# Gate rows, residual inputs and second-residual rows loaded some steps before use; second residual cut into eight pieces

## The chip, the cores and the metric

The kernel runs on one core of a Trainium2 chip. The metric is the device time of one execution in microseconds (us), as the median of several runs. The notation is that of the profile: PE is TensorE (matmul), PEld its weight loads, DVE is VectorE, ACT is ScalarE, POOL is GpSimd, SP is SyncE, which here only issues DMA transfers; a name with a q behind it (SPq) is the engine's own instruction queue. "L849" is line 849 of the kernel.

## The reference, cut to what matters

One encoder block over 512 positions of width 2048, in float32:

```
mod  = silu(c) @ w_ada + b_ada           # shift1, scale1, gate1, shift2, scale2, gate2, each of width 2048
z    = (x*(1+scale1) + shift1) @ w_in + b_in
mix  = (sigmoid(ga) * (A(z) @ w_a) + sigmoid(gb) * (B(z) @ w_b)) @ w_o + b_o
x    = LN1(alpha*x + gate1*mix)
x    = LN2(alpha*x + gate2*(relu((x*(1+scale2)+shift2) @ w_m1 + b_m1)**2 @ w_m2 + b_m2))
```

The part at stake is what joins the matmuls of w_o to the first matmuls of w_m1: the first residual (alpha*x + gate1*mix, with b_o folded in), its norm, and the start of the second residual (alpha*x with x the output of LN1 including its gain and bias, plus gate2*b_m2), to which the products of w_m2 are then added.

## The kernel before, in words

Every matrix is cut into blocks of 256 rows by 512 columns, and each block is one step `kp` of a group of output columns `cg`. The values are float32 kept as a pair of rounded halves (hi and lo), so that a product takes three matmuls (hi*hi, hi*lo, lo*hi). A block's way to TensorE is: SP loads it into a `wraw` buffer (512 KB, three buffers), ScalarE writes `whi` (L76), VectorE writes `wlo` (L77), three buffers each, and then come the matmuls of that step: 24 of 512 columns where four tiles of 128 positions are done, 24 of 256 columns where half the positions are done (`tok_0`, `tok_1`), 12 of 512 columns where two tiles are done. `Weights.take(k)`, called at the start of step k, gives out block k and emits the split of block k+2 and the load of a later one; so `wlo` of block k+2 stands on VectorE ahead of all that the stages of step k emit, and behind all that earlier steps emitted. Each engine works through its own queue in the order in which the program emits it, SP's transfers too.

`stages` is a table by hand: `stages={2: [f]}` calls f after the matmuls of step 2 have been emitted. The order around the change is this:

1. The last group of w_a (L773 to L778) with `parts` (splitting the mix into hi and lo pairs for w_o), then sums of the modulation vector (`mod_sum`), the last four `parts`, an activation that loads the table for the square root (L787), and small vectors for LN1.
2. `gate_rows` (L801): the columns gate1 and gate2 are copied (ScalarE, L804 and L805), turned into rows by one TensorE transpose (L807), copied from PSUM (L809) and stored to a buffer in HBM, `grow`. From there they are loaded again, spread over 128 partitions: `g1_row` (two loads of 512 KB) and `cond` (1 MB, gate2).
3. `residual(c)` (L828), for each of four column blocks c: load b_o's row (spread over the partitions, 256 KB) and x's four tiles (256 KB each), scale the row and multiply it by gate1, and add it to x, all on GpSimd: six instructions.
4. The groups c = 0 and c = 1 of w_o with four tiles (`token_dense`, L837, matmuls at L849), eight steps each, `gated_1` (L854) behind each: three VectorE instructions a tile. Then c = 2 and 3 for the first two tiles (`early`) and for the last two (`late`), with the norm and the transposes of LN1 in their stages.
5. The first group of w_m1 by halves of the positions (`tok_0`, `tok_1`, matmuls at L187), the second group (cg 1) with four tiles; `hidden` (L940) behind each: relu and square, two instructions a tile on ScalarE and two on VectorE. In the steps 0, 2, 4 and 6 of cg 1 stands `skip_path(c)` (L904) for c = 0 to 3: three rows are loaded, one product on GpSimd, nine instructions on VectorE.
6. The four groups of w_m2's first slab (L849, four steps each), then slab after slab without anything of the above.

`slot` tiles (128x512 float32, 39 buffers) hold x, rows, hidden values and intermediates alike. PSUM has 8 banks, handed out in turn.

Of the kernel before, what the change touches and what calls it, by code (L numbers as in the profile page):

```python
# [14 lines left out]
OP = mybir.AluOpType  # L15
# [3 lines left out]
P = 128  # L19
D = 2048  # L20
# [9 lines left out]
ALPHA = 2.0 ** 0.25  # L30
# [10 lines left out]
def block_kernel(ctx: ExitStack, tc: tile.TileContext, t):  # L41
    nc = tc.nc
# [11 lines left out]
    def slot(name, dt=F32):  # L54
        return heap.tile([P, 512], dt, name=name, tag="slot")

    def slot_pair(name):
        return slot(name + "h", F32R), slot(name + "l", F32R)
# [5 lines left out]
    def bank(name):  # L64
        return psum.tile([P, 512], F32, name=name, tag="bank")

    def f32(ap):
        return ap.bitcast(F32)

    def load(dst, src):  # L70
        nc.sync.dma_start(dst, src)  # L71
        return dst
# [121 lines left out]
    def dense(*args, **kw):  # L194
        out = []
        for _ in dense_steps(out, *args, **kw):
            pass
        return out
# [22 lines left out]
    cond = const.tile([P, D], F32, name="cond")  # L221
# [42 lines left out]
    grow = dram.tile([2, D], F32, name="grow")  # L264
# [354 lines left out]
    def do(f, *args):  # L619
        return lambda: f(*args)  # L620
# [24 lines left out]
    def merged(*parts):  # L645
        out = {}
        for p_ in parts:
            for k, v in p_.items():
                out.setdefault(k, []).extend(v)
        return out  # L650
# [94 lines left out]
    stages = {1 + i: [do(norm, 0, i)] for i in range(4)}  # L745
    stages.update({5: [do(norm, 1, 0)], 6: [do(norm, 1, 1), do(rows, 0)], 7: [do(norm, 1, 2), do(norm, 1, 3)]})
    sg = gate(0, 0, stages)
    for hf in range(2):
        stages = {k: [do(spatial, k // 3, i, mixed[k // 3]) for i in (2 * (k % 3) - 2, 2 * (k % 3) - 1)]
                  for k in (1, 2, 4, 5)} if hf == 0 else {}  # L750
# [12 lines left out]
    mp = []  # L763
# [6 lines left out]
    for cg in range(4):  # L770
        if cg:
            sg = gate(0, cg)
        ps = dense(t["w_a"], cg, 4, Ap,  # L773
                   stages={k: [do(parts, 3 * k + j) for j in range(3)] for k in range(4)} if cg == 3 else None)
# [23 lines left out]
    TILES = range(4)  # L798
    COLS = [slice(512 * c, 512 * (c + 1)) for c in range(4)]

    def gate_rows():  # L801

        both = small.tile([P, 2, KC], F32, name="gcols", tag="gcols")
        nc.scalar.copy(both[:, 0], mod[:, 2])  # L804
        nc.scalar.copy(both[:, 1], mod[:, 5])  # L805
        ps = bank("gT")
        nc.tensor.transpose(ps[:2 * KC, :P], both.rearrange("p g k -> p (g k)"), ident)  # L807
        rows_ = slot("gT")
        nc.scalar.copy(rows_[:2 * KC, :P], ps[:2 * KC, :P])  # L809
        for i in range(2):  # L810
            nc.sync.dma_start(grow[i].rearrange("(k p) -> k p", p=P), rows_[i * KC:(i + 1) * KC, :P])

    def row(src, name="row"):
        return load(slot(name), src.broadcast_to([P, 512]))

    gate_rows()
    g1_row = [wts.tile([P, 1024], F32, name="g1row", tag="araw") for _ in range(2)]
    for i, g in enumerate(g1_row):
        load(g, grow[0:1, 1024 * i:1024 * (i + 1)].broadcast_to([P, 1024]))
    load(cond, grow[1:2].broadcast_to([P, D]))  # L820
    g1_row = [g1_row[c // 2][:, c % 2 * 512:(c % 2 + 1) * 512] for c in range(4)]
    g2_row = [cond[:, s] for s in COLS]

    r = [[None] * 4 for _ in TILES]
    st1 = const.tile([P, 4, 4, 6], F32, name="st1")
    st2 = const.tile([P, 4, 4, 6], F32, name="st2")

    def residual(c):  # L828

        gb = row(t["rows"][0:1, COLS[c]])  # L830
        nc.gpsimd.tensor_scalar(gb, gb, 1.0 / ALPHA, None, op0=OP.mult)
        nc.gpsimd.tensor_tensor(gb, gb, g1_row[c], op=OP.mult)
        for i in TILES:
            r[i][c] = load(slot("r"), t["x"][i][:, COLS[c]])
            nc.gpsimd.tensor_tensor(r[i][c], r[i][c], gb, op=OP.add)

    def token_dense(w, cg, pairs, act, tiles=TILES, stages=None):  # L837

        out = {i: bank("t") for i in tiles}
        for kp in range(pairs):  # L840
            hi, lo = weights.take(w, cg, kp)
            for j in range(2):
                kc = 2 * kp + j
                ah, al = act[kc]
                c = slice(512 * j, 512 * (j + 1))
                for i in tiles:
                    s = slice(i * P, (i + 1) * P)
                    for m, (a, b) in enumerate(((ah[:, s], hi[:, c]), (ah[:, s], lo[:, c]), (al[:, s], hi[:, c]))):
                        nc.tensor.matmul(out[i], a, b, start=kc == 0 and m == 0, stop=kc == 2 * pairs - 1 and m == 2)  # L849
            for f in (stages or {}).get(kp, ()):  # L850
                f()
        return out

    def gated_1(ps, c, tiles=TILES):  # L854
        for i in tiles:
            x = slot("gated")
            nc.vector.tensor_tensor(x, ps[i], g1_row[c], op=OP.mult)
            nc.vector.scalar_tensor_tensor(r[i][c], r[i][c], ALPHA, x, op0=OP.mult, op1=OP.add)
            nc.vector.bn_stats(st1[:, i, c], r[i][c])
# [16 lines left out]
    h2 = []  # L876
# [24 lines left out]
            hi, lo = (x[:, tok] for x in h2[kc + k])  # L901
            split(h[:, 256 * k:256 * (k + 1)], hi, lo)

    def skip_path(c):  # L904

        g, b, m = (row(t["rows"][k:k + 1, COLS[c]]) for k in (1, 2, 3))
        nc.gpsimd.tensor_tensor(m, m, g2_row[c], op=OP.mult)
        nc.vector.scalar_tensor_tensor(b, b, ALPHA, m, op0=OP.mult, op1=OP.add)
        for i in TILES:
            nc.vector.scalar_tensor_tensor(r[i][c], r[i][c], ALPHA, g, op0=OP.mult, op1=OP.mult)  # L910
            nc.vector.tensor_tensor(r[i][c], r[i][c], b, op=OP.add)  # L911

    w_o = t["w_o"]
    early, late = (0, 1), (2, 3)
    tok_0, tok_1 = HALVES
    mom, held = {early: [], late: []}, []

    def norm_stages(tiles, first):

        out = {first: [lambda: mom[tiles].append(moments(st1, tiles)), do(normal_1, mom[tiles], tiles, 0)]}  # L920
        for k in range(1, 4):
            out.setdefault(first + k, []).append(do(normal_1, mom[tiles], tiles, k))
        return out

    residual(0)
    gated_1(token_dense(w_o, 0, 8, mp, stages={2: [do(residual, 1)]}), 0)
    gated_1(token_dense(w_o, 1, 8, mp, stages={2: [do(residual, 2)], 5: [do(residual, 3)]}), 1)
    for tiles in (early, late):
        for c in (2, 3):
            stages = {}  # L930
            if tiles is late and c == 2:
                stages = norm_stages(early, 1)
                for n in range(8):
                    stages.setdefault(2 + n * 3 // 4, []).append(do(turned, early, 2 * n, held))
            elif tiles is late:
                stages = {1 + n: [do(second_input, early, 2 * n, held)] for n in range(7)}
# [3 lines left out]
    def hidden(ps, n0, f, tok=ALL):  # L940
        for i in range(4):
            n = n0 + i
            if len(f) <= i + n0 % SLAB:
                f.append(slot_pair("f"))
            fh, fl = (x[:, tok] for x in f[i + n0 % SLAB])
            x = slot("relu")[:, tok]
            nc.scalar.activation(x, ps[i], AF.Relu, bias=bm1[:, n:n + 1], scale=1.0)
            nc.scalar.activation(fh, x, AF.Square)  # L948
            nc.vector.tensor_tensor(x, x, x, op=OP.mult)  # L949
            nc.vector.tensor_tensor(fl, x, f32(fh), op=OP.subtract)  # L950
# [14 lines left out]
    w1, w2 = t["w_m1"], t["w_m2"]  # L965
    n1 = SLAB // 4
    for s in range(NSLAB):
        f = []
        if s:
            for cg in range(n1):  # L970
                hidden(dense(w1, s * n1 + cg, 8, h2), SLAB * s + 4 * cg, f)
        else:
            stages = merged({0: [do(second_input, early, KC - 2, held)]}, norm_stages(late, 0))
            for n in range(8):
                stages.setdefault(2 + n * 3 // 4, []).extend([do(turned, late, 2 * n, held), do(second_input, late, 2 * n, held)])
            hidden(dense(w1, 0, 8, h2, tok_0, stages=stages), 0, f, tok_0)
            hidden(dense(w1, 0, 8, h2, tok_1), 0, f, tok_1)
            hidden(dense(w1, 1, 8, h2, stages={2 * c: [do(skip_path, c)] for c in range(4)}), 4, f)
        if s < NSLAB - 1:
            for cg in range(4):  # L980
                gated_2(token_dense(w2, 4 * s + cg, SLAB // 2, f), cg)
            continue
        gated_2(token_dense(w2, 4 * s, SLAB // 2, f), 0, stats=True)
        ln2_g = [row(t["rows"][4:5, COLS[c]], "ln2") for c in range(4)]
        ln2_b = [wts.tile([P, 1024], F32, name="ln2b", tag="araw") for _ in range(2)]
        for i, g in enumerate(ln2_b):
            load(g, t["rows"][5:6, 1024 * i:1024 * (i + 1)].broadcast_to([P, 1024]))
        ln2_b = [ln2_b[c // 2][:, c % 2 * 512:(c % 2 + 1) * 512] for c in range(4)]
        gated_2(token_dense(w2, 4 * s + 1, SLAB // 2, f), 1, stats=True)
        for i in TILES:  # L990
            for c in (2, 3):
                gated_2(token_dense(w2, 4 * s + c, SLAB // 2, f, (i,)), c, (i,), stats=True)
            last_norm(i, (0, 2) if i < 3 else (1,))
# [93 lines left out]
```

## Time and profile before

| | before |
|---|---|
| median of 3 runs | 2807.25 us (2804.49 to 2808.98) |
| the profiled execution | 2811.11 us |
| its span, first to last instruction | 2809.3 us |
| TensorE busy | 2719.5 us (97%) |
| VectorE busy | 1537.2 us (55%) |
| ScalarE busy | 788.8 us (28%) |
| GpSimd busy | 149.7 us (5%) |
| mean granted TensorE clock | 0.986 |

The span is the time between the first and the last recorded instruction; the execution's own time is 1.8 us more. A busy share is the time in which the engine had an instruction running. Matmuls are recorded with about 0.39 us each, but follow each other every 0.227 us, since they are pipelined; their pace is read from the starts.

### The profile page before, as it was taken

Reading aid. Unit: us, or ns where it says so; the run is one execution under the profiler, and the core shown is the slowest. Engines: PE = TensorE matmul, PEld = TensorE weight load, DVE = VectorE, ACT = ScalarE, POOL = GpSimd, SP = SyncE. Lnnn points to the kernel's source line nnn. Section 1 sums busy time; section 2 is a strip of 40 time slices with the busy share of each in tenths; the row PEclk is TensorE's granted clock in tenths of the full one; section 3 lists DMA queues with packets and bytes.
Section 4 is the critical chain, followed back from the end, with each engine's and each line's share of the span. In section 5 each row is a group of like instructions: output and inputs, shape, how many; then the busy total and the mean of one; then the engine's idle time right before and its main releaser. Section 6 shows DMA issues by size and latency. Waiting matters only on the chain.

```text
span 2809.3 us, 29794 instructions
## 1 busy us (share of the span) xinstructions
PE 2719.5 (97%) x11909; PEld 2204.5 (78%) x11909; DVE 1537.2 (55%) x2032; ACT 788.8 (28%) x965; POOL 149.7 (5%) x99
## 2 busy tenths in 40 slices
PE   6999999999999999999979999999999999999996
PEld 2487777888888888778957888888888888888885
DVE  8966978554566556446735444344343533434348
ACT  3334323222223222324621221222212222132232
POOL 6610000000000000130000000000000000000001
PEclk9899999999999999999989999999999999999998
DMA  9673332555565567435542232322322232223242
GB/s 303 227 279 114 125 105 98 195 194 194 197 213 185 194 219 260 151 128 180 174 104 93 95 98 97 98 98 90 105 98 98 90 100 97 98 96 98 98 138 80
DMA packets 120475, 400.45 MB, mean 143 GB/s; under 512 B 14283, under 2 KB 14315, under 8 KB 120208
## 3 DMA queue, kind: packets, MB, share of 16 engines
q1 hardware_dynamic: 120336, 398.55, 42.6%
q8 instruction: 93, 1.52, 0.2%
q14 instruction: 46, 0.38, 0.0%
HBM read 388.00 MB, written 10.50 MB: 142 GB/s over the span
## 4 chain that ended last, share of the span: by engine, by line
PE 84%; DVE 5%; DMA 3%; ACT 1%; issue 1%; SPq 0%; POOL 0%; DVEq 0%; ACTq 0%; POOLq 0%
PE d L187 54%; PE t L849 28%; DMA row<-in_rows 1%; DVE wlo L77 1%; DMA xT<-in_xT 1%; PE inv L611 1%; PE inv L599 0%; DMA wraw<-in_w_m 0%; ACT whi L76 0%; DVE r L960 0%; DVE r L962 0%; DVE r L910 0%; DVE r L865 0%; SPq L71 0%; DVE r L911 0%
## 5 line engine op out<-in xcount | busy, mean ns | idle before, releaser
L187 PE MATMUL d<-act,whi 128*128 128x512 f32 (+1 forms) x4224 | 1283.0, 386 | 3.9 <-DVE bf_e L308 1.5
L77 DVE TENSOR_TENSOR wlo<-wraw,whi 128x1024 fp32r<-128x1024 f32 x480 | 587.9, 1229 | 1032.3 <-ACT whi L76 1032.0
L76 ACT CAST whi<-wraw 128x1024 fp32r<-128x1024 f32 x480 | 504.6, 1054 | 1564.4 <-PE d L187 931.9
L187 PEld LDWEIGHTS d<-act,whi 128*128 128x128 f32 x4224 | 786.5, 189 | 167.8 <-issue 7.2
L187 PE MATMUL d<-act,wlo 128*128 128x512 f32 (+1 forms) x2112 | 812.5, 385 | 20.4 <-DVE wlo L77 20.4
L187 PEld LDWEIGHTS d<-act,wlo 128*128 128x128 f32 x2112 | 398.8, 189 | 101.1 <-DVE wlo L77 22.8
L849 PE MATMUL t<-wlo,fh 128*128 128x512 f32 x960 | 374.8, 390 | 5.9 <-DVE wlo L77 5.9
L849 PE MATMUL t<-whi,fl 128*128 128x512 f32 x960 | 374.5, 390 | 0.0
L849 PE MATMUL t<-whi,fh 128*128 128x512 f32 x960 | 374.4, 390 | 0.0
L253 DVE SCALAR_TENSOR_TENSOR araw<-araw,cond 128x1024 f32<-128x1024 f32 x192 | 254.3, 1345 | 8.3 <-DMA araw<-in_ada 8.3
L849 PEld LDWEIGHTS t<-wlo,fh 128*128 128x128 f32 x960 | 180.8, 188 | 43.9 <-DVE wlo L77 6.4
L849 PEld LDWEIGHTS t<-whi,fl 128*128 128x128 f32 x960 | 180.9, 188 | 37.7
L849 PEld LDWEIGHTS t<-whi,fh 128*128 128x128 f32 x960 | 180.8, 188 | 37.7
L849 PE MATMUL t<-whi,act 128*128 128x512 f32 x512 | 162.5, 397 | 0.0
L849 PEld LDWEIGHTS t<-whi,act 128*128 128x128 f32 x512 | 98.2, 192 | 20.6
L864 DVE TENSOR_TENSOR gated<-t,cond 128x512 f32<-128x512 f32 x128 | 87.6, 684 | 31.6 <-PE t L849 31.6
L849 PE MATMUL t<-wlo,act 128*128 128x512 f32 x256 | 101.5, 397 | 2.4 <-DVE wlo L77 2.4
L865 DVE TENSOR_TENSOR r<-r,gated 128x512 f32<-128x512 f32 x128 | 88.6, 692 | 4.4
L962 POOL TENSOR_TENSOR r<-r,ln2b 128x512 f32<-128x512 f32 x7 | 11.6, 1663 | 1316.4 <-DVE r L960 1315.1
L187 PE MATMUL d<-whi,act 128*128 128x512 f32 x256 | 78.9, 389 | 0.0
L949 DVE TENSOR_TENSOR relu<-relu 128x512 f32<-128x512 f32 (+1 forms) x68 | 44.6, 656 | 38.8 <-ACT fh L948 38.8
L387 POOL TENSOR_TENSOR flt<-flt,win 128x512 f32<-128x512 f32 x32 | 63.7, 2018 | 6.7 <-ACT flt L385 5.9
(204 smaller groups left out, 1935.9 us busy)
## 6 DMA issues: line engine op xcount, KB each, us to landing
wraw<-in_w_m SPq DMA_DIRECT2D x264, 512.0 KB, 3.5
araw<-in_ada SPq DMA_DIRECT2D x192, 512.0 KB, 4.8
wraw<-in_w_in SPq DMA_DIRECT2D x144, 512.0 KB, 3.5
wraw<-in_w_o SPq DMA_DIRECT2D x48, 512.0 KB, 3.5
spec<-spec SPq DMA_DIRECT2D x48, 256.0 KB, 4.9
wraw<-in_w_b SPq DMA_DIRECT2D x16, 512.0 KB, 3.4
wraw<-in_w_a SPq DMA_DIRECT2D x16, 512.0 KB, 3.6
xT<-in_xT SPq DMA_DIRECT2D x16, 256.0 KB, 5.3
```

The source lines that it names most:

```text
L76: nc.scalar.copy(hi, src)
L77: nc.vector.tensor_tensor(lo, src, f32(hi), op=OP.subtract)
L187: nc.tensor.matmul(out[i], a, b, start=first and m == 0, stop=last and m == 2)
L253: nc.vector.scalar_tensor_tensor(raw, raw, 1.0, cond[:, 1024 * h:1024 * (h + 1)], op0=OP.mult, op1=OP.mult, accum_out=dots[:, m, kc, h:h + 1])
L387: nc.gpsimd.tensor_tensor(x, x, win, op=OP.mult)
L611: nc.tensor.matmul(ps[:, cl * P:(cl + 1) * P], conv.y[cl][cs][:, s], ic(4 * cs + COLUMN[cl]), start=(cs == 0), stop=(cs == 1))
L849: nc.tensor.matmul(out[i], a, b, start=kc == 0 and m == 0, stop=kc == 2 * pairs - 1 and m == 2)
L864: nc.vector.tensor_tensor(x, ps[i], g2_row[c], op=OP.mult)
L865: nc.vector.tensor_tensor(r[i][c], r[i][c], x, op=OP.add)
L949: nc.vector.tensor_tensor(x, x, x, op=OP.mult)
L962: eng.tensor_tensor(x, x, ln2_b[c], op=OP.add)
```

## The change

Four things are moved or cut.

- `gate_rows` and the loads of its rows (`gate_loads`) go from the place ahead of w_o into the steps 1 and 3 of group c = 0.
- `residual` is split into `residual_load` (the five loads) and the GpSimd arithmetic. The loads for c = 0 stand ahead of w_o, those for c = 1 in step 4 of group 0, for c = 2 and 3 in steps 0 and 4 of group 1; the arithmetic in step 5 of group 0 and in steps 0, 3 and 6 of group 1.
- `skip_path` is split into `skip_rows` (three loads), `skip_bias` (the bias row alpha*b + gate2*m, now wholly on GpSimd: three instructions instead of one there and one on VectorE) and `skip_path(c, i)` (two VectorE instructions for one tile).
- `skip_rows(c)` stands two steps ahead of the first tiles of c, `skip_bias(c)` one step ahead (for c = 0 in the steps 3 and 6 of the `tok_1` group), and the tiles go two and two into the steps 2c and 2c+1 of cg 1: eight pieces of four instructions instead of four of nine.

```diff
-    gate_rows()
     g1_row = [wts.tile([P, 1024], F32, name="g1row", tag="araw") for _ in range(2)]
-    for i, g in enumerate(g1_row):
-        load(g, grow[0:1, 1024 * i:1024 * (i + 1)].broadcast_to([P, 1024]))
-    load(cond, grow[1:2].broadcast_to([P, D]))
+
+    def gate_loads():
+        for i, g in enumerate(g1_tiles):
+            load(g, grow[0:1, 1024 * i:1024 * (i + 1)].broadcast_to([P, 1024]))
+        load(cond, grow[1:2].broadcast_to([P, D]))
+
+    g1_tiles = g1_row
...
-    def residual(c):
-
-        gb = row(t["rows"][0:1, COLS[c]])
-        nc.gpsimd.tensor_scalar(gb, gb, 1.0 / ALPHA, None, op0=OP.mult)
-        nc.gpsimd.tensor_tensor(gb, gb, g1_row[c], op=OP.mult)
+    def residual_load(c):
+        gb.append(row(t["rows"][0:1, COLS[c]]))
         for i in TILES:
             r[i][c] = load(slot("r"), t["x"][i][:, COLS[c]])
-            nc.gpsimd.tensor_tensor(r[i][c], r[i][c], gb, op=OP.add)
+
+    def residual(c):
+
+        b = gb[c]
+        nc.gpsimd.tensor_scalar(b, b, 1.0 / ALPHA, None, op0=OP.mult)
+        nc.gpsimd.tensor_tensor(b, b, g1_row[c], op=OP.mult)
+        for i in TILES:
+            nc.gpsimd.tensor_tensor(r[i][c], r[i][c], b, op=OP.add)
...
-    def skip_path(c):
-
-        g, b, m = (row(t["rows"][k:k + 1, COLS[c]]) for k in (1, 2, 3))
+    def skip_rows(c):
+        skips.append([row(t["rows"][k:k + 1, COLS[c]]) for k in (1, 2, 3)])
+
+    def skip_bias(c):
+
+        g, b, m = skips[c]
         nc.gpsimd.tensor_tensor(m, m, g2_row[c], op=OP.mult)
-        nc.vector.scalar_tensor_tensor(b, b, ALPHA, m, op0=OP.mult, op1=OP.add)
-        for i in TILES:
-            nc.vector.scalar_tensor_tensor(r[i][c], r[i][c], ALPHA, g, op0=OP.mult, op1=OP.mult)
-            nc.vector.tensor_tensor(r[i][c], r[i][c], b, op=OP.add)
+        nc.gpsimd.tensor_scalar(b, b, ALPHA, None, op0=OP.mult)
+        nc.gpsimd.tensor_tensor(b, b, m, op=OP.add)
+
+    def skip_path(c, i):
+        g, b, _ = skips[c]
+        nc.vector.scalar_tensor_tensor(r[i][c], r[i][c], ALPHA, g, op0=OP.mult, op1=OP.mult)
+        nc.vector.tensor_tensor(r[i][c], r[i][c], b, op=OP.add)
...
-    residual(0)
-    gated_1(token_dense(w_o, 0, 8, mp, stages={2: [do(residual, 1)]}), 0)
-    gated_1(token_dense(w_o, 1, 8, mp, stages={2: [do(residual, 2)], 5: [do(residual, 3)]}), 1)
+    residual_load(0)
+    gated_1(token_dense(w_o, 0, 8, mp, stages={1: [gate_rows], 3: [gate_loads], 4: [do(residual_load, 1)],
+                                               5: [do(residual, 0)]}), 0)
+    gated_1(token_dense(w_o, 1, 8, mp, stages={0: [do(residual, 1), do(residual_load, 2)], 3: [do(residual, 2)],
+                                               4: [do(residual_load, 3)], 6: [do(residual, 3)]}), 1)
...
-            hidden(dense(w1, 0, 8, h2, tok_1), 0, f, tok_1)
-            hidden(dense(w1, 1, 8, h2, stages={2 * c: [do(skip_path, c)] for c in range(4)}), 4, f)
+            hidden(dense(w1, 0, 8, h2, tok_1, stages={3: [do(skip_rows, 0)], 6: [do(skip_bias, 0)]}), 0, f, tok_1)
+            stages = {}
+            for c in range(4):
+                for at, fs in ((2 * c - 2, [do(skip_rows, c)]), (2 * c - 1, [do(skip_bias, c)]),
+                               (2 * c, [do(skip_path, c, i) for i in (0, 1)]),
+                               (2 * c + 1, [do(skip_path, c, i) for i in (2, 3)])):
+                    if at >= 0:
+                        stages.setdefault(at, []).extend(fs)
+            hidden(dense(w1, 1, 8, h2, stages=stages), 4, f)
```

## Rows read from the trace of the kernel before

**Rows 1.** TensorE's waits, 1140 to 1500: releaser, us in total, times, longest.

```profile
PE d L187 <- DVE wlo L77: 18.3, 4, 6.9
PE t L849 <- DVE wlo L77: 8.4, 2, 5.9
PE gT L807 <- ACT gcols L805: 6.2, 1, 6.2
```

**Rows 2.** TensorE's timeline, 1159 to 1265: start, us, what [idle before].

```profile
1159.56 0.39 PE L187 MATMUL d<-Ah,wlo 128*128 128x512 f32 x1
1166.15 0.40 PE L807 MATMUL gT<-ident,gcols 128*32 128x128 f32 x1 [6.21 <-ACT gcols L805]
1166.20 0.78 PE L849 MATMUL t<-whi,act 128*128 128x512 f32 x1
...
1171.89 0.41 PE L849 MATMUL t<-wlo,act 128*128 128x512 f32 x1
...
1264.29 0.80 PE L849 MATMUL t<-wlo,act 128*128 128x512 f32 x1 [2.44 <-DVE wlo L77]
```

**Rows 3.** TensorE's timeline, 1403 to 1568.

```profile
1403.73 0.63 PE L187 MATMUL d<-act,whi 128*128 128x512 f32 x2
...
1425.84 0.80 PE L187 MATMUL d<-act,wlo 128*128 128x512 f32 x1 [5.15 <-DVE wlo L77]
...
1445.08 0.79 PE L187 MATMUL d<-act,wlo 128*128 128x512 f32 x1 [5.50 <-DVE wlo L77]
...
1464.71 0.79 PE L187 MATMUL d<-act,wlo 128*128 128x512 f32 x1 [6.89 <-DVE wlo L77]
...
1483.52 0.79 PE L849 MATMUL t<-wlo,fh 128*128 128x512 f32 x1 [5.93 <-DVE wlo L77]
...
1567.77 0.62 PE L187 MATMUL d<-act,whi 128*128 128x512 f32 x2
```

**Rows 4.** Chain that ended last, a later slab: start, us, what.

```profile
1567.93 87.04 PE d L187 x384
```

**Rows 5.** Windows: length, busy us (instructions) by engine, granted clock, DMA share, GB/s.

```profile
1386.00:1404.00 18.00, 17.41 (x144) 17.37 (x145) 9.13 (x9) 7.52 (x10) 0.00 (x0) 1.00 0.61 206
1425.00:1445.00 20.00, 13.74 (x48) 10.81 (x48) 8.90 (x13) 2.10 (x2) 1.30 (x1) 0.76 0.37 92
```

**Rows 6.** VectorE's timeline, 1391 to 1490.

```profile
1391.62 1.23 DVE L77 TENSOR_TENSOR wlo<-wraw,whi 128x1024 fp32r<-128x1024 f32 x1 [2.81 <-ACT whi L76]
...
1419.25 0.69 DVE L910 SCALAR_TENSOR_TENSOR r<-r,row 128x512 f32<-128x512 f32 x1
...
1424.57 2.35 DVE L77 TENSOR_TENSOR wlo<-wraw,whi 128x1024 fp32r<-128x1024 f32 x2
...
1483.38 0.68 DVE L949 TENSOR_TENSOR relu<-relu 128x512 f32<-128x512 f32 x1
...
1488.70 2.35 DVE L77 TENSOR_TENSOR wlo<-wraw,whi 128x1024 fp32r<-128x1024 f32 x2
```

**Rows 7.** Timelines of SP's queue and of GpSimd, around 1410.

```profile
1408.82 1.37 SPq L71 DMA_DIRECT2D row<-in_rows  x3
1417.31 1.29 POOL L907 TENSOR_TENSOR row<-row,cond 128x512 f32<-128x512 f32 x1 [160.11 <-DMA row<-in_rows]
```

**Rows 8.** Timelines of ScalarE, VectorE and SP's queue around the start of w_o.

```profile
1136.18 2.73 ACT L678 ACTIVATE sg<-d,c_bin 128x512 f32<-128x512 f32 x4 [2.57 <-PE d L187]
1167.82 1.23 DVE L77 TENSOR_TENSOR wlo<-wraw,whi 128x1024 fp32r<-128x1024 f32 x1
1168.23 0.82 SPq L71 DMA_DIRECT2D g1row<-grow  x2
```

**Rows 9.** Instructions on the tile `row`: ns min/median/max, first and last start.

```profile
L835 POOL TENSOR_TENSOR r<-r,row x16: 1282/1296/2356, 1180.0 to 1255.4; 128x512 f32<-128x512 f32 x16
L831 POOL TENSOR_SCALAR row<-row x4: 1488/1492/1495, 1177.1 to 1247.7; 128x512 f32<-128x512 f32 x4
```

**Rows 10.** VectorE's timeline where GpSimd runs beside it.

```profile
1197.47 1.87 DVE L77 TENSOR_TENSOR wlo<-wraw,whi 128x1024 fp32r<-128x1024 f32 x1 [4.09 <-ACT whi L76]
```

More of the change, by code (lines that the diff above doesn't have):

```diff
@@ L826, in block_kernel @@
     st2 = const.tile([P, 4, 4, 6], F32, name="st2")
-    def residual(c):
-        gb = row(t["rows"][0:1, COLS[c]])
-        nc.gpsimd.tensor_scalar(gb, gb, 1.0 / ALPHA, None, op0=OP.mult)
-        nc.gpsimd.tensor_tensor(gb, gb, g1_row[c], op=OP.mult)
+    def residual_load(c):
+        gb.append(row(t["rows"][0:1, COLS[c]]))
         for i in TILES:
             r[i][c] = load(slot("r"), t["x"][i][:, COLS[c]])
-            nc.gpsimd.tensor_tensor(r[i][c], r[i][c], gb, op=OP.add)
+    def residual(c):
[4 more added lines that the diff above has]
+            nc.gpsimd.tensor_tensor(r[i][c], r[i][c], b, op=OP.add)
+    gb = []
     def token_dense(w, cg, pairs, act, tiles=TILES, stages=None):
@@ L902, in second_input @@
             split(h[:, 256 * k:256 * (k + 1)], hi, lo)
-    def skip_path(c):
-        g, b, m = (row(t["rows"][k:k + 1, COLS[c]]) for k in (1, 2, 3))
+    def skip_rows(c):
+        skips.append([row(t["rows"][k:k + 1, COLS[c]]) for k in (1, 2, 3)])
+    def skip_bias(c):
+        g, b, m = skips[c]
         nc.gpsimd.tensor_tensor(m, m, g2_row[c], op=OP.mult)
-        nc.vector.scalar_tensor_tensor(b, b, ALPHA, m, op0=OP.mult, op1=OP.add)
-        for i in TILES:
-            nc.vector.scalar_tensor_tensor(r[i][c], r[i][c], ALPHA, g, op0=OP.mult, op1=OP.mult)
-            nc.vector.tensor_tensor(r[i][c], r[i][c], b, op=OP.add)
+        nc.gpsimd.tensor_scalar(b, b, ALPHA, None, op0=OP.mult)
[4 more added lines that the diff above has]
+        nc.vector.tensor_tensor(r[i][c], r[i][c], b, op=OP.add)
+    skips = []
     w_o = t["w_o"]
```

## The prediction

> **What bounds the kernel now.** The table of the profile comes first: TensorE is busy for 97% of the span, so a change away from TensorE pays only where TensorE stands still. The waits of TensorE over the stretch that the diff touches come next: about 33 us, nearly all for a late `wlo`, and once for `gcols`, that is, for the transpose inside `gate_rows` [rows 1]. TensorE's own timeline then shows what each wait costs. In later slabs 384 matmuls take 87.04 us, 0.227 us each [rows 4], so a step of 24 takes 5.44 us and a group of eight steps 43.5 us. I compare each stretch with this pace.
>
> Behind a wait the pace is worse for a while. The first w_o matmul starts at 1166.20 and the fourteenth at 1171.89: 5.69 us for 13 intervals where 2.95 are needed, so 2.74 us are lost after the gap too [rows 2]. The 20 us window from 1425 shows a mean granted clock of 0.76 [rows 5]. Gaps therefore cost their length and some 2 to 3 us more.
>
> **Part one, the start of w_o.** The last w_a matmul starts at 1159.56, so TensorE is free at 1159.79. Next in its queue is the transpose, which waits for ScalarE and VectorE to finish the mix and the modulation sums; w_o starts at 1166.20 [rows 2]. After the change the transpose stands behind step 1. What the first two steps need (the splits of blocks 0 and 1, the first pairs of the mix) was emitted during w_a and is done. I take their PSUM banks to be those of the last gate group, whose reading ended at 1138.9 [rows 8]; that the four banks of w_a are taken instead is a rival below. So w_o starts at 1159.8, and the gap of 6.41 us and the 2.74 us behind it go.
>
> What is late next: the split of block 2, at 1167.82 + 1.23 = 1169.05 [rows 8], is wanted at 1159.8 + 2 x 5.44 = 1170.7. It holds by 1.6 us, and the table load and the small vectors ahead of it don't move. The transpose now costs its slot, 0.05 us from its start to the next matmul, or 0.4 us by its record at the most [rows 2]; I take 0.1. Its input is copied by ScalarE behind the split of block 3, some 2 us before TensorE comes to it. **Gain: 6.41 + 2.74 - 0.1 = 9.1 us.**
>
> The rows' way is longer now, and is hidden by group 0's matmuls. SP issues `gate_loads` behind the load of step 3, at about 1179. Before, the rows were issued at 1168.2 [rows 8] and used before 1180.0, when the first add of x began [rows 9], so they land in under 11.8 us, now by 1190.8. GpSimd then needs 1.49 + 1.29 + 4 x 1.3, some 8 us [rows 7, 9], up to 1199. `gated_1` wants the sum at 1159.8 + 43.5 - 1.2 = 1202. The load of x for c = 0 has from 1158 on; the others have more than a step each. If a sum came late, `gated_1` would hold VectorE and the next `wlo` with it. SP's moved loads put 3.25 MB ahead of weight blocks whose use is three steps (16 us) off.
>
> The gap of 2.44 us at 1264 [rows 2] stays: it comes from the `gated_1` of c = 1 standing ahead of a split. GpSimd's last adds (the last starts at 1255.4 [rows 9]) ran beside that `gated_1`, and end earlier now, which can only help. I take nothing for it, and 4 us, gap and slow pace, as the end of the range below.
>
> **Part two, cg 1 of w_m1.** It starts at 1403.73, and the next slab starts at 1567.77 [rows 3]: 164.04 us for 192 + 384 matmuls, which need 576 x 0.2267 = 130.6. **Lost: 33.5 us**, in the four gaps at 1425.84, 1445.08, 1464.71 and 1483.52 [rows 3] and the slow pace behind each. Each gap is one `skip_path`: SP issues its rows at 1408.82 and GpSimd starts at 1417.31, 8.5 us later [rows 7], with VectorE held in its queue; then come nine instructions, and only at 1424.57 the splits that TensorE wants [rows 6].
>
> After the change the rows of c are issued two steps before their use. The chain is 8.5 us from issue to GpSimd (one weight load ahead of them in both cases), then 1.29 + 1.49 + 1.29 and starts between, 4.2 us [rows 7, 9]: 12.7 us. On VectorE a piece takes half of 1424.57 - 1419.25, 2.66 us, a split 1.2 us, `hidden` 1488.70 - 1483.38 = 5.3 us [rows 6]. With step k of cg 1 at 1403.73 + 5.44k, in order:
>
> The rows of c = 0 leave behind the split of step 3 of `tok_1`, 1391.62 + 1.23 [rows 6], at 1392.9; their bias is done near 1406, and the first piece runs from 1408.4 on. Rows 1 leave at 1408.8, bias 1421.5; the piece ends at 1424.2, and the split for step 5 is done at 1425.4, wanted at 1430.9. Rows 2 leave at 1417.5, bias 1430.2; the split for step 7 is done at 1434.1, wanted at 1441.8. Rows 3 leave behind two more pieces and splits at 1429.7, bias 1442.4; the last two pieces, `hidden` and three splits follow, and the split for step 2 of w_m2's first group is done at 1455.5, wanted at 1403.73 + 10 x 5.44 = 1458.1. The splits between hold by 7 us and more. The least margin is thus 2.6 us, and no gap is left. VectorE has some 31 us of work in the 43.5 us of cg 1. **Gain: 33.5 us.**
>
> In `tok_1` the transfers already run at 206 GB/s [rows 5], and the rows of c = 0 put 0.75 MB among them. If they take 8.5 us as at 1408.82, they have landed at 1401.4; the weight load behind them, 0.5 MB at that rate, lands 2.5 us later, and with some 2.4 us for the two halves of its split block 1 of cg 1 is ready near 1406.3. It is wanted at 1409.2: hidden, by 2.9 us.
>
> One instruction fewer a block on VectorE (four of 0.69 us) and two more on GpSimd cost nothing as long as these margins hold.
>
> **The sum.** 9.1 + 33.5 = 42.6 us off the profiled execution's 2811.1 gives 2768.5. That execution is 3.9 us above the median of the runs, so on the median it is 2807.25 - 42.6 = **2764.6 us**, 1.5% faster.
>
> **A rule against it.** GpSimd now computes the bias beside VectorE. The rows show a split at 1.87 us while GpSimd added rows, instead of 1.23 [rows 8, 10], so up to 0.64 us a meeting; three meetings make 1.9 us, which the margin of 2.6 us holds. The Trainium skill, page "SBUF — State Buffer", section "Who interferes with whom", says that VectorE with two SBUF inputs and GpSimd share a read port as an exclusive lock, the later one waiting for the other's whole instruction. By that, three meetings would cost up to 4.1 us and the margin would be gone.
>
> **The rivals.** *The chain of rows 3 is late* (chance 12%). For it: the least margin, 2.6 us, at the end of a chain of eleven links, and VectorE and GpSimd meeting along it; GpSimd's add was once 2.36 us [rows 9]. Against: GpSimd runs the last bias while VectorE waits for it. It decides at 2.6 us; a delay of 4.1 us leaves 1.5 us and a slow pace of up to 2.8: 2769.
>
> *The rows crowd out the weights in `tok_1`* (4%). A delay past the 2.9 us margin costs a gap of 1 us and a slow pace behind it: 2768.
>
> *Part one does nothing, or half* (6%): w_o's first bank, or a split, is free only later, so the gap changes its name. Nothing in the waits names a bank, and group 1 follows group 0 without a gap. At worst 9.1 us are lost: 2774.
>
> *The row loads wait for buffers* (4%). If rows of c+1 had to wait until those of c are free, SP would hold them, and each c would take in series 12.7 + 0.4 + two pieces and a split, 6.5: 19.6 us. From 1415.0, where the first c is done, three such periods, `hidden` and a split end at 1480.3, 22.2 us late, and with three spells of slow pace 29: 2794. It turns slower than before where the period passes 24.1 us, which is about reached with three GpSimd instructions of 2.36 us [rows 9], the split at 1.87 [rows 10] and rows 1 us later (24.3): 2808. Against: x holds 16 of 39 buffers, half the hidden values 8, two sets of rows 6. I give 1.5% to slower by over 0.2% (5.6 us, about what a measurement can tell from no change) and as much to no change.
>
> **How the numbers follow.** The forecast has 74%, 2760 to 2768 by itself: the 4 us at 1264, and the spread of the runs of 2 to 3 us either way. The range goes down to 2758 (both together, nearly) and up to 2776, over the first three rivals; the last one and a second failing are left out, under 10%. Faster 97%, same 1.5%, slower 1.5%.
>
> **What would show it.** Right: no wait of TensorE on `gcols`; w_o starting within 1 us of the last w_a matmul; no gap over 1 us between the start of cg 1 and the end of w_m2's first slab, 130.6 us later; a granted clock of 1.00 over both; the wait at 1264 still there. Wrong: a wait of TensorE for `wlo` at step 2 of w_m2's first group (rival one), in `tok_1` or step 1 of cg 1 (rival two), for something else before w_o (rival three), or SP waiting for VectorE's pieces (rival four).

## The result, and the profile after

The changed kernel takes 2768.11 us (median, 2765.17 to 2769.61), the one before 2807.47 us in the same comparison: a ratio of 0.986, with an interval of 0.9843 to 0.9877, so 34 to 44 us less. The forecast was 42.6 us less, 2764.6 us. The profiled execution of the changed kernel took 2768.32 us against 2811.11 us, 42.8 us less; the medians differ by 39.4 us, within the interval. One of the five executions of run l below took 3904.39 us at a mean granted clock of 0.656 (0.992 in the others); its median of 2765.36 us counts it, and the other four alone give 2765.00 us.

TensorE's waits in the changed kernel, over the stretch of [rows 1] (releaser, us in total, times, longest):

```profile
PE t L858 <- DVE wlo L77: 2.1, 1, 2.1
PE d L187 <- DVE wlo L77: 0.8, 1, 0.8
PE h2T L898 <- DVE r L889: 0.5, 2, 0.3
```

Of 33 us of waiting, 3.4 are left, and the wait on `gcols` is gone. TensorE's timeline shows where, in the places of [rows 2, 3]:

```profile
1158.20 0.39 PE L187 MATMUL d<-Ah,wlo 128*128 128x512 f32 x1
1158.43 0.39 PE L858 MATMUL t<-whi,act 128*128 128x512 f32 x1
...
1169.08 0.39 PE L858 MATMUL t<-whi,act 128*128 128x512 f32 x1
1169.31 0.27 PE L807 MATMUL gT<-ident,gcols 128*32 128x128 f32 x1
1169.34 0.48 PE L858 MATMUL t<-whi,act 128*128 128x512 f32 x1
...
1253.52 0.50 PE L858 MATMUL t<-wlo,act 128*128 128x512 f32 x1 [2.08 <-DVE wlo L77]
...
1393.06 0.63 PE L187 MATMUL d<-act,whi 128*128 128x512 f32 x2
...
1447.49 0.39 PE L858 MATMUL t<-whi,fh 128*128 128x512 f32 x1
1447.92 0.50 PE L858 MATMUL t<-wlo,fh 128*128 128x512 f32 x1
...
1524.00 0.62 PE L187 MATMUL d<-act,whi 128*128 128x512 f32 x2
```

w_o follows w_a at the usual pace of 0.227 us, and the transpose lies between two of its matmuls. cg 1 and the first slab of w_m2 take 1524.00 - 1393.06 = 130.94 us instead of 164.04; the only irregular place is 1447.49 to 1447.92, 0.43 us where 0.227 is usual. The windows give the clock (columns as in [rows 5]):

```profile
1392.00:1437.00 45.00, 45.00 (x205) 37.45 (x204) 33.18 (x44) 14.57 (x21) 18.06 (x12) 1.00 0.53 169
1437.00:1524.00 87.00, 86.95 (x384) 71.65 (x383) 46.18 (x57) 19.55 (x21) 0.00 (x0) 1.00 0.31 103
```

Cut at the end of w_a (its last matmul plus 0.227 us), the start of cg 1 and the start of the second slab, the executions compare so (us):

| | w_a's end to cg 1 | cg 1 to second slab | second slab to the end of the span |
|---|---|---|---|
| before | 243.94 | 164.04 | 1241.53 |
| changed | 234.63 | 130.94 | 1242.50 |

The stretches of the change give 9.3 + 33.1 = 42.4 us. What lies outside them differs by under 1.4 us each way (w_a ends 1.36 us earlier, what follows takes 0.97 us more).

### The profile page after: what moved, and what is told of

It is laid out like the page before. It is cut to its first block, busy times and chain, and to the rows that moved or that the text cites. A ratio compares the mean times of both kernels' runs of the same rounds, so it can differ in the third digit from the quotient of the medians.

```text
span 2766.5 us, 29801 instructions
## 1 busy us (share of the span) xinstructions
PE 2705.7 (98%) x11909; PEld 2196.0 (79%) x11909; DVE 1538.4 (56%) x2028; ACT 788.3 (28%) x965; POOL 162.9 (6%) x107
## 3 DMA queue, kind: packets, MB, share of 16 engines
q1 hardware_dynamic: 120336, 398.55, 42.8%
q8 instruction: 93, 1.52, 0.2%
## 4 chain that ended last, share of the span: by engine, by line
PE 90%; DVE 5%; DMA 2%; issue 1%; ACT 1%; POOL 1%; SPq 0%; DVEq 0%; ACTq 0%; POOLq 0%
PE d L187 57%; PE t L858 28%; PE flt L383 1%; DVE araw L253 1%; DVE wlo L77 1%; DMA araw<-in_ada 1%; PE inv L611 1%; PE inv L599 0%; DMA wraw<-in_w_m 0%; PE f_o L324 0%; PE f_ee L312 0%; PE f_eo L316 0%; DVE r L979 0%; DVE r L981 0%; DVE r L874 0%
## 5 line engine op out<-in xcount | busy, mean ns | idle before, releaser
L839 POOL TENSOR_SCALAR row<-row 128x512 f32<-128x512 f32 x4 | 6.2, 1539 | 977.8 <-DVE mod L259 956.3
```

Source lines behind the costliest of these rows:

```text
L839: nc.gpsimd.tensor_scalar(b, b, 1.0 / ALPHA, None, op0=OP.mult)
```

## The experiments

The theory was that TensorE lost its time in two places to in-order queues: to a transpose standing in its own queue, and to splits standing behind VectorE's wait for rows. The rivals said that the crowd of transfers, the length of the pieces on VectorE, or GpSimd's work cost it. The table gives the times; a stretch is read as above.

| run | median, us | ratio to before, interval | w_a's end to cg 1 | cg 1 to second slab |
|---|---|---|---|---|
| a: part one alone | 2796.43 | 0.9965 (0.9952 to 0.9977) | 233.05 | 160.59 |
| b: part two alone | 2776.98 | 0.9897 (0.9883 to 0.991) | 245.49 | 130.68 |
| c: rows early, pieces whole | 2766.31 | 0.9857 (0.9844 to 0.9871) | 234.64 | 130.59 |
| d: pieces, rows late | 2800.10 | 0.9982 (0.9973 to 0.9992) | 233.01 | 162.39 |
| e: rows one step ahead | 2786.08 | 0.9922 (0.9907 to 0.9937) | 233.00 | 149.15 |
| f: bias on VectorE | 2767.56 | 0.9856 (0.9842 to 0.9871) | 234.62 | 131.06 |
| g: one split first | 2768.21 | 0.9857 (0.9842 to 0.9872) | 233.00 | 130.59 |
| h: transpose in front | 2777.32 | 0.9891 (0.9874 to 0.9907) | 241.60 | 132.33 |
| i: loads with arithmetic | 2771.73 | 0.9872 (0.9857 to 0.9888) | 236.24 | 131.33 |
| j: first rows earlier | 2769.19 (one run) | - | 234.68 | 130.58 |
| k: gated_1 spread | 2765.97 | 0.9849 (0.9836 to 0.9863) | 230.65 | 131.53 |
| l: all of it | 2765.36 | 0.9848 (0.9834 to 0.9861) | 231.44 | 130.59 |

### a and b: each part alone

Run a is the changed kernel with the old `skip_path` and its old stages, run b the old kernel with the new ones.

> Part one alone: the changed start of w_o, with the old skip_path. My theory (the transpose standing in TensorE's queue costs a gap of 6.4 us and the slow pace behind it): 9.1 to 9.3 us less than the kernel before, a ratio of 0.9967; from the last w_a matmul to the first of cg 1 some 234.6 us as in the changed kernel, then the four gaps of before, 164 us from there to the next slab. Rival (the two parts help each other, for example through a shared queue of transfers): less than 7 us or more than 12 us.

> Part two alone: the changed skip path with the old start of w_o. My theory: 33.1 to 33.5 us less than before, a ratio of 0.988, with the wait on gcols of 6.2 us still there. Rival (the parts depend on each other): the two single gains don't add up to the 42.4 us of both parts.

Part one alone: 2806.01 - 2796.43 = 9.6 us. In its stretch it is 243.94 - 233.05 = 10.9 us instead of 9.3, since the gap at the start of c = 2 has no slow pace behind it in this execution. Part two alone: 29.0 us by the medians (25 to 33 by the interval), less than the 33.1 to 33.5 that I expected, and 33.4 us in its stretch (164.04 - 130.68). The stretch of part one is 1.55 us longer in b than before, since the gap at the start of c = 2 is 3.0 us there instead of 2.4 and the slow pace behind it costs 2.8 us instead of 1.6. The parts add up, 38.6 us by the medians against 39.4 for both, and neither needs the other. TensorE's waits of run b show the one that part one removes:

```profile
PE gT L807 <- ACT gcols L805: 6.2, 1, 6.2
PE t L849 <- DVE wlo L77: 3.0, 1, 3.0
```

Run a also suggests why the medians give less for part two than the profile. Its cg 1 runs the `skip_path` of before, but the stretch is 160.59 us, not 164.04. From the issue of a set of rows to GpSimd's product it takes 7.9 to 8.5 us in run a, 32.7 us for the four sets, and 8.5 to 9.6 us in the profiled execution of before, 36.1 us: 3.4 us of difference, as in the stretch. The third set before, and then in run a:

```profile
1446.61 2.18 SPq L71 DMA_DIRECT2D row<-in_rows  x3
1456.17 1.30 POOL L907 TENSOR_TENSOR row<-row,cond 128x512 f32<-128x512 f32 x1 [18.33 <-DMA row<-in_rows]
```

```profile
1432.72 1.92 SPq L71 DMA_DIRECT2D row<-in_rows  x3
1441.18 1.30 POOL L916 TENSOR_TENSOR row<-row,cond 128x512 f32<-128x512 f32 x1 [17.22 <-DMA row<-in_rows]
```

Against run a's stretch part two is worth 160.59 - 130.94 = 29.7 us, near the 29.0 of the medians. There is no trace of a median execution of before, so whether part one also shortens the way of the rows stays open.

### c and d: early rows or even pieces

```diff
 c:
-                               (2 * c, [do(skip_path, c, i) for i in (0, 1)]),
-                               (2 * c + 1, [do(skip_path, c, i) for i in (2, 3)])):
+                               (2 * c, [do(skip_path, c, i) for i in TILES])):
 d:
-                for at, fs in ((2 * c - 2, [do(skip_rows, c)]), (2 * c - 1, [do(skip_bias, c)]),
-                               (2 * c, [do(skip_path, c, i) for i in (0, 1)]),
+                for at, fs in ((2 * c, [do(skip_rows, c), do(skip_bias, c)] + [do(skip_path, c, i) for i in (0, 1)]),
```

In d the rows of c = 0 leave `tok_1` too.

> The changed kernel with the rows early but all four tiles of c in step 2c, so four pieces of eight instructions instead of eight of four. My theory (what TensorE waited for is the way of the rows: load, GpSimd, with VectorE held behind it; the pieces themselves fit): within 1 us of the changed kernel, no gap in cg 1. Rival (the length of one piece on VectorE holds the split, so the cutting pays): four pieces of 5.3 us bring gaps of 1 us and more back, 2771 us and above.

> The changed kernel with the eight pieces kept, but the rows of c loaded and the bias computed in the same step 2c in which the first piece stands. My theory: the gaps are back. A period of rows 8.5, GpSimd 4.2, two pieces and two splits 7.7, SP 0.4 us makes 20.8 us instead of 18.5 to 19.6 before: 2798 to 2806 us, four gaps. Rival (the even pieces alone let the splits through): most of the 33 us stay, under 2780 us.

Run c has no gap in cg 1 (130.59 us, the pace of 0.2267 alone) and the time of the changed kernel. Run d has the gaps back; TensorE's timeline in it:

```profile
1411.93 0.50 PE L187 MATMUL d<-act,wlo 128*128 128x512 f32 x1 [2.99 <-DVE wlo L77]
...
1430.98 0.79 PE L187 MATMUL d<-act,wlo 128*128 128x512 f32 x1 [6.27 <-DVE wlo L77]
...
1450.59 0.79 PE L187 MATMUL d<-act,wlo 128*128 128x512 f32 x1 [5.78 <-DVE wlo L77]
...
1469.18 0.79 PE L858 MATMUL t<-wlo,fh 128*128 128x512 f32 x1 [6.15 <-DVE wlo L77]
```

So part two comes from the early rows, and four whole pieces do as well as eight. With late rows the eight pieces bring nothing either: run a, with late rows and four whole pieces, takes 2796.43 us and 160.59 in the stretch, run d 2800.10 and 162.39. Run d also has the longer chain on GpSimd (three instructions a block instead of one), so what the cutting does with late rows isn't separated from that.

### e: how much lead is needed

```diff
-                for at, fs in ((2 * c - 2, [do(skip_rows, c)]), (2 * c - 1, [do(skip_bias, c)]),
+                for at, fs in ((2 * c - 1, [do(skip_rows, c), do(skip_bias, c)]),
```

The rows and bias of c = 0 stand in step 7 of `tok_1`.

> The changed kernel with the rows loaded one step ahead of the first piece instead of two (the bias in the same step as its rows). My theory by the same chain of numbers: the bias of c = 1 is done at +21.7 us from the start of cg 1 and holds; the one of c = 2 comes too late by some 4.5 us and that of c = 3 by 4 us, each with 2 us of slow pace: 10 to 15 us more than the changed kernel, 2778 to 2783 us. Rival (the margins are larger than I reckon, rows land sooner with fewer transfers ahead): under 2771 us, no gap.

It costs 18 us, more than I reckoned. SP's timeline shows the sets of rows leaving 16.5 and 16.1 us apart where two steps are 10.9 us:

```profile
1409.30 1.37 SPq L71 DMA_DIRECT2D row<-in_rows  x3
1412.71 13.03 SPq L71 DMA_DIRECT2D wraw<-in_w_m  x2
1425.83 1.33 SPq L71 DMA_DIRECT2D row<-in_rows  x3
1429.20 12.72 SPq L71 DMA_DIRECT2D wraw<-in_w_m  x2
1441.97 1.37 SPq L71 DMA_DIRECT2D row<-in_rows  x3
```

These are the rows of c = 1, 2 and 3. SP's own waits from 1390 to 1460, and VectorE's timeline for c = 1:

```profile
SPq L71 <- DVE wlo L77: 57.1, 9, 12.3
```

```profile
1413.93 0.69 DVE L925 SCALAR_TENSOR_TENSOR r<-r,row 128x512 f32<-128x512 f32 x1 [1.24 <-DMA row<-in_rows]
1422.23 0.69 DVE L926 TENSOR_TENSOR r<-r,row 128x512 f32<-128x512 f32 x1 [7.61 <-POOL row L921]
```

From rows to bias it takes 1422.23 - 1409.30 = 12.9 us, as forecast (12.7). But a held piece delays the split behind it, that split frees the buffer for the next weight load (SP's waits are for `wlo`), and the next rows stand behind that load in SP's queue: the lateness is handed on to every later c. It begins with c = 0, for whose bias VectorE waits 7.5 us, so the bias of c = 1 is done at +29.2 us from the start of cg 1 (1392.98) and not at +21.7. I had let each c start anew.

### f: the bias on VectorE

```diff
-        nc.gpsimd.tensor_scalar(b, b, ALPHA, None, op0=OP.mult)
-        nc.gpsimd.tensor_tensor(b, b, m, op=OP.add)
+        nc.vector.scalar_tensor_tensor(b, b, ALPHA, m, op0=OP.mult, op1=OP.add)
```

> The changed kernel with the bias row finished on VectorE in one instruction, as before, instead of two on GpSimd. My theory (off the path that sets the end): the same time within 1 us, and the bias done 2 us earlier. Rival (GpSimd beside VectorE costs by the shared port): up to 0.4 us faster, since the changed kernel loses 0.4 us against the full pace in cg 1.

Same time. VectorE now waits for the rows a step earlier, and the irregular place at step 2 of w_m2 stays (131.06 us). It stays although GpSimd lengthens no VectorE instruction in cg 1 here (those of a piece take 0.68 or 0.69 us). Moving the bias to GpSimd neither pays nor costs.

### h and i: what part one consists of

Run h calls `gate_rows()` ahead of `residual_load(0)` again. Run i loads and adds in one step:

```diff
+    def both(c):
+        residual_load(c)
+        residual(c)
+
+    gated_1(token_dense(w_o, 0, 8, mp, stages={1: [gate_rows], 3: [gate_loads], 5: [do(both, 0)]}), 0)
+    gated_1(token_dense(w_o, 1, 8, mp, stages={0: [do(both, 1)], 3: [do(both, 2)], 6: [do(both, 3)]}), 1)
```

> The changed kernel with gate_rows alone put back ahead of w_o; the loads stay moved. My theory (the transpose in TensorE's queue is the whole of part one): 9 us more than the changed kernel, the wait on gcols of 6.2 us back. Rival (the crowd of transfers and the GpSimd work at the start of w_o cost it): within 2 us of the changed kernel.

> The changed kernel with the five loads of each residual put back into the step of its arithmetic (steps 5, 0, 3 and 6), the transpose and the gate loads staying moved. My theory (the loads of x were hidden anyway; only the transpose paid in part one): within 1 us of the changed kernel, although the first sum is done some 2 us after gated_1 wants it, since the split behind it has 3 us to spare. Rival (the lead of the loads is needed): gated_1 of c = 0 waits, and a gap of 3 us or more with its slow pace stands near the start of group 1, 2773 us and above.

Run h is 9.2 us slower than the changed kernel, with the wait on `gcols` back at 6.2 us:

```profile
1164.13 0.39 PE L807 MATMUL gT<-ident,gcols 128*32 128x128 f32 x1 [6.21 <-ACT gcols L805]
...
1455.58 0.50 PE L858 MATMUL t<-wlo,fh 128*128 128x512 f32 x1 [1.40 <-DVE wlo L77]
```

Not all of the 9.2 us belong to part one: 1.4 us in the second stretch are the wait at step 2 of w_m2's first group. The first stretch is 7.0 us longer, although the gap at the start of c = 2 has no slow pace here, which saves 1.6. The transpose with the slow pace behind it thus costs 8.6 us, nearly all of part one's 9.3.

Run i misses my theory, by 2.0 us in the two stretches and 3.6 us by the medians (the intervals overlap). The sum for c = 0 was no trouble. The gap stands at the end of group 1, where VectorE works on `gated_1` of c = 1 while GpSimd still adds for c = 3. TensorE, VectorE and GpSimd there:

```profile
1255.78 0.80 PE L858 MATMUL t<-wlo,act 128*128 128x512 f32 x1 [3.86 <-DVE wlo L77]
```

```profile
1246.39 0.67 DVE L866 TENSOR_TENSOR gated<-t,g1row 128x512 f32<-128x512 f32 x1
1247.17 1.65 DVE L867 SCALAR_TENSOR_TENSOR r<-r,gated 128x512 f32<-128x512 f32 x1
1248.85 0.69 DVE L868 BATCH_NORM_STATS2 st<-r 128x6 f32<-128x512 f32 x1
...
1250.24 1.52 DVE L867 SCALAR_TENSOR_TENSOR r<-r,gated 128x512 f32<-128x512 f32 x1
```

```profile
1246.98 5.92 POOL L842 TENSOR_TENSOR r<-r,row 128x512 f32<-128x512 f32 x4
```

Two VectorE instructions with both inputs in SBUF lose 1.79 us beside GpSimd, while those that read PSUM or write statistics lose nothing; the gap grows by 1.78 us, from 2.08 to 3.86. So the early loads of x do pay a little, not by being in time but by ending GpSimd's work before `gated_1` begins.

### j: where the margin went

The split for step 2 of w_m2's first group came 0.2 us late, where I had forecast 2.6 us to spare. Run j moves the first rows and their bias out of `tok_1`:

```diff
+                stages[2].extend([do(skip_rows, 0), do(skip_bias, 0)])        # last group of w_o
-            hidden(dense(w1, 0, 8, h2, tok_1, stages={3: [do(skip_rows, 0)], 6: [do(skip_bias, 0)]}), 0, f, tok_1)
+            hidden(dense(w1, 0, 8, h2, tok_1), 0, f, tok_1)
```

> The changed kernel with the rows and the bias of c = 0 moved from tok_1 to step 2 of the last w_o group. It asks why the margin of 2.6 us at step 2 of w_m2's first group was found at about zero. Theory A (the rows of c = 0 crowd out a weight load in tok_1, the relus behind it are late, and all later rows leave 3.4 us late): the wait of 5 us for that load goes, the third rows leave at +27 to +28 us from the start of cg 1 instead of +30.7, and the split stands ready 2 us or more before it is wanted. Theory B (VectorE and GpSimd meeting, 2.4 us in all, eat the margin): the third rows leave at +29.5 us or later and the margin stays under 1 us.

In the changed kernel ScalarE, SP, GpSimd and VectorE show:

```profile
1393.43 1.05 ACT L76 CAST whi<-wraw 128x1024 fp32r<-128x1024 f32 x1 [5.00 <-DMA wraw<-in_w_m]
1394.38 0.47 ACT L966 ACTIVATE relu<-d,c_bm 128x256 f32<-128x256 f32 x1
```

```profile
1401.60 1.33 SPq L71 DMA_DIRECT2D row<-in_rows  x3
...
1423.73 1.37 SPq L71 DMA_DIRECT2D row<-in_rows  x3
```

```profile
1395.06 1.83 POOL L921 TENSOR_TENSOR row<-row 128x512 f32<-128x512 f32 x1
```

```profile
1395.65 1.52 DVE L968 TENSOR_TENSOR relu<-relu 128x256 f32<-128x256 f32 x1
...
1417.07 1.78 DVE L925 SCALAR_TENSOR_TENSOR r<-r,row 128x512 f32<-128x512 f32 x1
1418.89 0.98 DVE L926 TENSOR_TENSOR r<-r,row 128x512 f32<-128x512 f32 x1
...
1420.51 1.68 DVE L926 TENSOR_TENSOR r<-r,row 128x512 f32<-128x512 f32 x1
...
1446.65 3.49 DVE L77 TENSOR_TENSOR wlo<-wraw,whi 128x1024 fp32r<-128x1024 f32 x3
```

and SP and VectorE in run j:

```profile
1420.98 2.65 SPq L71 DMA_DIRECT2D row<-in_rows  x3
```

```profile
1444.88 2.36 DVE L77 TENSOR_TENSOR wlo<-wraw,whi 128x1024 fp32r<-128x1024 f32 x2
```

Counted from the start of cg 1 (1393.06 changed, 1394.41 in j), the third rows of cg 1 (those of c = 3) leave at +30.7 and at +26.6 us, and the split that TensorE wants at +54.4 is done some 1.2 us after its start, at +54.8 and at +51.7. The meetings of VectorE and GpSimd on the pieces are much the same in both (1.78 and 1.68 us in one, three of 1.77 to 1.79 in the other). Theory A holds in the main: with the rows of c = 0 out of `tok_1`, a margin of 2.7 us is there, as forecast. One meeting has a share in it: in the changed kernel the sum for the bias of c = 0 meets the first relu on VectorE, 1.52 us instead of 0.42. The rows of c = 1 leave 3.4 us later than in j (+8.5 and +5.1), of which some 2.4 are the late weight load and 1.1 this meeting; both go with the rows of c = 0.

It brings no time, since the gap was 0.2 us, and j has a new gap of 1.4 us in `tok_0`, right behind the last w_o group, where the rows now stand:

```profile
1348.52 0.39 PE L187 MATMUL d<-act,wlo 128*128 128x256 f32 x1 [1.41 <-DVE wlo L77]
```

### g, k and l: the gap that is left

The gap at 1253 comes from a split standing behind `gated_1`. Run g emits the split first and moves two of its four tiles into step 1 of the next group; run k moves three tiles, one each into the steps 1, 3 and 5:

```diff
-    gated_1(token_dense(w_o, 1, 8, mp, stages={0: [do(residual, 1), do(residual_load, 2)], 3: [do(residual, 2)],
-                                               4: [do(residual_load, 3)], 6: [do(residual, 3)]}), 1)
+    second = token_dense(w_o, 1, 8, mp, stages={0: [do(residual, 1), do(residual_load, 2)], 3: [do(residual, 2)],
+                                               4: [do(residual_load, 3)], 6: [do(residual, 3)],
+                                               7: [weights.prepare]})
+    gated_1(second, 1, (0,))                  # g: early
...
+            elif c == 2:
+                stages = {2 * i - 1: [do(gated_1, second, 1, (i,))] for i in (1, 2, 3)}   # g: {1: [do(gated_1, second, 1, late)]}
```

Run l is k with the edit of j and `weights.prepare` in step 7 of `tok_0`.

> The changed kernel with one split emitted ahead of gated_1 of c = 1, and the second half of that gated_1 in step 1 of the next group. My theory (the 2.1 us gap at 1253 comes from the split that stands behind gated_1 on VectorE): the gap goes with its slow pace, 3.5 to 4.2 us less than the changed kernel. Rival (the next split or the norm is then late): the gap moves to a later step and the gain is under 1 us.

> The changed kernel with one split emitted ahead of gated_1 of c = 1 and the tiles 1, 2 and 3 of that gated_1 put into the steps 1, 3 and 5 of the next group, one at a time. My theory (a step of that group is 2.7 us of TensorE, so VectorE can take one split and one tile in it, and not two tiles): the gap of 2.1 us goes, 2 to 4 us less than the changed kernel. Rival (as with two tiles at once, the gap only moves on): 2 us of waiting for a split are seen a step or two later, and the time is that of the changed kernel.

> The version that the runs point to: the changed kernel with the rows of c = 0 loaded in the last w_o group, gated_1 of c = 1 spread over three steps, and a split emitted ahead of hidden at the end of tok_0. My theory: no wait of TensorE over 0.5 us between the start of w_o and the second slab; 2.1 and 0.8 us of gaps, 0 to 1.6 us of slow pace and 0.4 us in cg 1 go, so 3 to 5 us less than the changed kernel, 2762 to 2765 us. Rival (the gaps move elsewhere): under 1.5 us less.

In g the gap only moves, from step 2 to step 4 of the group, as TensorE's timeline shows:

```profile
1259.79 0.50 PE L858 MATMUL t<-wlo,act 128*128 128x512 f32 x1 [2.03 <-DVE wlo L77]
```

A step there is 2.7 us, and two tiles (4.2 us) with a split (1.2 us) don't fit into two steps with all that follows. In k, one tile at a time, the gap is gone and the stretch is 230.65 us, 4.0 us shorter than in the changed kernel, of which some 1.7 are the slow pace behind the gap; against a, d and e, where the gap has none, it is 2.4 us shorter. The wait at step 2 of w_m2's first group is 0.64 us in k. In l the stretch is 231.44, with a gap of 1.67 us at the place of j's, so my expectation of no wait over 0.5 us missed. Over both stretches k and l take 362.2 and 362.0 us, the changed kernel 365.6. By the medians they are 2.1 and 2.8 us faster than the changed kernel; the intervals of their ratios overlap with its own, so that gain is shown in the stretches and not yet by the times.

## Why the prediction was right, and where it was off

**Part one**, forecast 9.1 us: 9.3 us in the profile, 9.6 us alone by the medians. That the profile comes within 0.2 us is partly luck: the gap at the start of c = 2 had its slow pace in this execution, and without it the same stretch is 1.6 us shorter (run a). The gap of 6.41 us is gone, the banks were free, and the split of block 2 came in time. The transpose costs 0.03 us between its start and the next matmul. The gate rows were in use at 1183.6 and GpSimd's first sum was done at 1191, 8 us before the bound that I took.

**Part two**, forecast 33.5 us: 33.1 us in the profile, but 29.0 us alone by the medians. The mechanism was right: all four gaps went, and the chain from rows to bias (12.7 forecast) takes 12.9 us in run e and 11.8 to 12.4 in the changed kernel. The term was some 4 us too large, for the reason given below on the whole.

**The step that failed** is the margin: 2.6 us forecast, none found. In `tok_1` I followed the late weight load as far as the split behind it, forecast for 2.6 us after the start of cg 1 and found at 2.7 (1394.51 + 1.23 - 1393.06), and called it hidden. I did not follow what stands behind that split: the relus of `hidden` on ScalarE, the next split, and with it the rows that SP sends. The rows of c = 1 left at +8.5 us instead of +5.1, those of c = 3 at +30.7 instead of +26.0. The first rival, a late chain at this very place, thus set in by 0.2 us, and by 1.4 us in run h.

**The meetings** of VectorE and GpSimd cost up to 1.1 us each (1.78 us for 0.685), not the 0.64 us that I took from one row of before; three of them added 2.4 us to the pieces in cg 1, and a fourth 1.1 us to a relu ahead of them. That is nearer to the exclusive lock of the Trainium skill, page "SBUF — State Buffer", section "Who interferes with whom". Run j has three such meetings on its pieces as well, and the forecast margin with them, so these alone did not take it.

**The gap at 1264** stayed, as forecast, 2.08 us instead of 2.44.

**The rivals.** Rows waiting for buffers didn't occur. The second rival's crowd in `tok_1` was there, but cost the margin and no gap in `tok_1` or step 1 of cg 1. The cutting into even pieces, which I had not priced by itself, is worth nothing here.

**The size of the whole** was forecast from one execution, at 42.6 us; its profile has 42.4 us in the two stretches. The medians differ by 39.4 us, within the interval of 34 to 44 us. The remaining 3 us fit a step that I took without a reason: the lost time of part two was read from an execution 3.9 us above the median, and taken off the median in full. The rows' way in that execution was 3.4 us longer than in run a, so its excess would lie in the very gaps that the change removes. There is a single trace of before, so this fits the numbers but isn't shown.

## What to carry to other kernels

What pays in a staged kernel is to keep an instruction that waits from standing ahead of one that the busy engine needs: one small transpose cost 9 us, and four sets of rows 33 us in the profile (29 by the medians), while cutting the arithmetic into pieces brought nothing once the rows came early. The lead must cover load, GpSimd and the work ahead of them in the queues, and a late set delays the next one through SP's queue, so one step too little cost 18 us. A late transfer may look hidden because the instruction that it delays is still in time; follow that engine's queue behind it all the same. And a loss read from one execution is that execution's: before it is taken off a median, it wants a second trace.

## What the runs showed of the hardware

- TensorE doesn't always fall to the slow pace after the same gap. After a wait of 2.07 or 2.08 us at the start of c = 2, seven or eight matmuls followed at 0.427 us in the changed kernel and in c and f, and in a, d, e, h and j they followed at 0.227 us throughout. The first stretch is 1.6 us longer in the former (234.6 against 233.0 in a, d and e). The granted clock over the slower matmuls is 0.50 to 0.52 in the former, the lower of the two levels, 1.2 GHz; right behind the same wait it is 1.00 in the latter, 2.4 GHz. In the changed kernel and in a (columns as in [rows 5]):

```profile
1255.30:1258.50 3.20, 3.20 (x9) 2.48 (x9) 0.43 (x1) 1.04 (x1) 0.00 (x0) 0.52 0.88 292
```

```profile
1253.60:1259.00 5.40, 5.40 (x24) 4.47 (x25) 2.89 (x3) 1.05 (x1) 0.00 (x0) 1.00 0.64 216
```

- A VectorE instruction of 0.69 us with both inputs in SBUF took up to 1.79 us beside GpSimd's instructions of 1.3 to 1.5 us, and a GpSimd product of 1.3 us up to 1.94 us in the changed kernel; a relu's product with itself took 1.52 us instead of 0.42. In run i the products that read PSUM (0.67 us) and the statistics of one tile (0.69 us) took no longer beside GpSimd.
- The way of three rows of 256 KB, from SP's issue behind weight loads to GpSimd's first instruction on them, took 7.9 to 9.6 us with the same code in run a and before.
